# Gate weights split one half-tile a row behind long exponentials, and queries loaded a head ahead, in a one-core conformer layer

## The chip, the cores and the metric

The kernel runs on one core of a Trainium2 chip. The metric is the device time of one execution in microseconds (us), lower is better. Three executions of the kernel before took 1444.28, 1443.33 and 1444.24 us, with a median of 1444.24 us.

## The reference

The kernel computes one inference step of a hybrid streaming encoder layer in float32: a prompt of 1024 frames and 32 new frames of a running stream with 512 cached keys. Model width 1024, 8 heads of 64, a convolution branch of 512 channels, and a feed-forward width of 4096.

```python
p = x @ w_in            # [GLU pair | q | k | v | forget logits | branch gates 2*1024]
u = a * sigmoid(b);  y_conv = swish(LN(causal depthwise conv_31(u))) @ w_conv_out
c = cumsum(log_sigmoid(p_f + b_f))
s = q @ k.T / 8 + c_q - c_k;  s = where(k_pos <= q_pos, s, -1e30)
o = softmax(s) @ v;  y_attn = o @ w_attn_out
mix = (sigmoid(g_conv) * y_conv + sigmoid(g_attn) * y_attn) @ w_o
x1 = LN1(alpha * x + mix);  x2 = LN2(alpha * x1 + relu(x1 @ w_up)**2 @ w_down)
```

## The kernel before

Every float32 matrix is split into a high and a low part, and a product is three matrix products that are summed in PSUM: high by high, high by low, low by high (`mm3`). So a weight tile of 128 x 1024 must be split before TensorE (PE) can use it. The class `Weights` (object `W`) does that. It loads a tile as two raw halves of 128 x 512 (names `raw60`, `raw61`, ...; four raw buffers), and for each half ScalarE (ACT) copies the high part (`whi30`) and another engine subtracts it from the raw half to get the low part (`wlo30`). During the attention that engine is GpSimd (POOL): `W.engine = "pool"`. Four tiles of parts can be held (`RB = 4`). `W.take` gives the next tile to a consumer and splits what is not yet split.

The order of the instructions on PE, ACT, VectorE (DVE) and POOL is written out by the kernel itself: class `Issue` (object `I`) keeps a modelled clock for each engine and emits instructions in the order in which the Python code reaches them. The order of SyncE's (SP's) transfers is set by the framework's scheduler. `I.service` is called after each group of work and first calls `I.always`, which is `W.ahead`: it loads raw halves as buffers allow and splits every half that has arrived and has a place.

The attention is the stage of `with pool("b")`. Its work units are 8 prompt heads with 8 rows each and 4 cached streams (two heads each, 544 keys), which stand behind heads 2, 3, 4 and 5. Row r (class `Rows`) is a block of 128 queries against n = (r + 1) * 128 keys, so a row has 128 to 1024 keys. The loop over units is a software pipeline of four stages. In one turn the newest row `a0` gets its scores on PE (`ps_s_<head>_<row>`, keys `k1`, `k2` and queries `q1`, `q2`) and its minimum on DVE; the row three turns back, `a3`, gets its product with v on PE (`ps_pv<head>_<pair>`, for odd rows), which ACT (`oa`, `ob`) and POOL (`oh`, `ol`) then drain; `a2` is transposed on PE (`ps_tr_<head>_<row>_<first key tile>`) and copied to its high part on ACT (`th`); `a0` gets its exponential on ACT (`p`, in `weigh`); `a1` is scaled by the reciprocal row sum on DVE (`p<-p,rs`, in `norm`); then DVE makes the low part of `a2`'s transposes (`tl`). The service call ends the turn.

PSUM has two buffers for scores (tag `s`), two shared by the transposes and the products with v (tag `tr`), and two for the gates (tag `acc`).

Between these steps PE gets filler: 6 matmuls at a time of the gate tiles 6 to 15 (`ps_g<tile>_<chunk>`) and of two early output tiles (`ps_yc`). `I.fill(needs)` stands ahead of scores, transposes and products. It emits filler while the model says that the needs are not ready, as long as a quota lasts that grows by some 1.7 groups a row. What the fillers take is split by `W` as above.

A cached stream's keys come as a raw array `ckr`. DVE casts its two heads into `k1` (`sk` in the trace), POOL subtracts the cast from it into `k2` (`k<-ckr,sk`), and the values go the same way over ACT and POOL. These steps are a background generator, `parts`, which `Stream.scores` flushes right before the stream's scores.

`load_head` issues a head's transfers, at row 2 of the head (or at the stream) before: `k1` (two transfers of 256 KB), `q1` (two of 256 KB), the low keys in `k2` (256 KB, and a small one), the high queries in `q2` (256 KB, and a small one), and `v` (512 KB). `k1`, `k2` and `v` alternate between two buffers from unit to unit, `q1` and `q2` from head to head. Head 0's transfers go over POOL's queue, all others over SP's.

The lines that decide when a half is split, before:

```python
def ahead(self):
    while len(self.raw) < 2 * self.limit and held["raw"] < RAWB:
        self.load()
    while self.halves < len(self.raw) and I.ready(self.raw[self.halves]) <= I.t["pe"] and \
            (self.halves % 2 or self.halves // 2 in kept or held["parts"] < RB):
        self.split()
        if len(self.raw) < 2 * self.limit:
            self.load()
```

Of the kernel before, what the change touches and what calls it, by code (L numbers as in the profile page):

```python
# [10 lines left out]
F32R = mybir.dt.float32r  # L11
# [6 lines left out]
P = 128  # L18
D = 1024
SEQ = 1024  # L20
# [5 lines left out]
NKS = PAST + DEC  # L26
# [3 lines left out]
H = 8  # L30
DH = 64
# [9 lines left out]
NT = SEQ // P  # L41
# [4 lines left out]
RB = 4  # L46
# [34 lines left out]
class Issue:  # L81
# [116 lines left out]
    def dma(self, out, in_, queue=None):  # L198
        self.run("dma", max(450, Issue.size(out) * out.shape[0] * 4 / 360), [out], [in_])
        out, in_ = (t.bitcast(F32) if t.dtype == F32R else t for t in (out, in_))  # L200
        (queue or self.nc.sync).dma_start(out, in_)
# [10 lines left out]
    def act(self, out, in_, func, bias=None, **kw):  # L212
        aps = [] if bias is None else [bias]
        self.run("act", self.size(in_) * 0.81 + (62 if self.psum(in_) else 103) + 93 * len(aps),
                 [out] + [v for k, v in kw.items() if k == "accum_out"], [in_] + aps)
        if bias is not None:
            kw["bias"] = bias
        self.nc.scalar.activation(out, in_, func, **kw)  # L218
# [5 lines left out]
    def tt(self, out, a, b, op, eng="dve"):  # L224
        n = self.size(out)
        self.run(eng, n * 1.01 + 80 if eng == "dve" else n * 1.97 + 150, [out], [a, b])
        (self.nc.vector if eng == "dve" else self.nc.gpsimd).tensor_tensor(out, a, b, op)  # L227
# [35 lines left out]
def f32(t):  # L263
    return t.bitcast(F32)
# [3 lines left out]
def hybrid_layer(ctx: ExitStack, tc, io):  # L268
    nc = tc.nc
    I = Issue(nc)  # L270
    dma, mm, act, cp, tt, ts, stt = I.dma, I.mm, I.act, I.cp, I.tt, I.ts, I.stt
# [13 lines left out]
    qk_s = {n: tc.dram_tile([H * DH, T], F32, name=f"{n}_s") for n in ("qh", "ql", "kh", "kl")}  # L285
# [27 lines left out]
    NWO = len(plan)  # L313
# [5 lines left out]
    held = dict(raw=0, parts=0)  # L319

    kept = {NWO + m: lambda m=m: [row(7 + m + n, f"{x}_wo{m}") for n, x in enumerate(("whi", "wlo"))] for m in range(1, KD, 2)}

    class Weights:
        def __init__(self):
            self.raw, self.parts, self.taken, self.done, self.halves = [], [], 0, 0, 0
            self.engine, self.limit = "dve", NWO + 1

        def load(self, queue=None):
            i = len(self.raw)
            held["raw"] += 1  # L330
            self.raw.append(ring.tile([P, RW // 2], F32, tag="raw", bufs=RAWB, name=f"raw{i}"))
            w = plan[i // 2]
            n = w.shape[1] // 2
            dma(self.raw[i][:, :n], w[:, i % 2 * n:(i % 2 + 1) * n], queue)
# [17 lines left out]
        def ahead(self):  # L352
            while len(self.raw) < 2 * self.limit and held["raw"] < RAWB:
                self.load()
            while self.halves < len(self.raw) and I.ready(self.raw[self.halves]) <= I.t["pe"] and \
                    (self.halves % 2 or self.halves // 2 in kept or held["parts"] < RB):
                self.split()
                if len(self.raw) < 2 * self.limit:
                    self.load()

        def take(self):
            self.ahead()
            i = self.taken
            while self.halves < 2 * i + 2:
                if len(self.raw) == self.halves:
                    self.load()
                self.split()
            self.taken += 1
            return self.parts[i]
# [6 lines left out]
    class Sums:  # L376
# [18 lines left out]
        def step(self):  # L395
            n = self.n
            self.n += 1
            u, o = divmod(n + 5, 7)
            if u < len(self.units):
                raw = [self.raw.get((u, i)) for i in range(4)]  # L400
                if o == 2:
                    self.total("s1", u, raw[1], raw[3], ADD)
                    self.total("s2", u, self.sums["s1", u], raw[0], SUB)
                if o == 4:
                    self.total("s3", u, raw[0], raw[1], SUB)
                    self.load(u + 1, 0)
                    self.load(u + 1, 1)
                if o == 5:
                    self.total("s4", u, raw[2], self.sums["s2", u], SUB)
                    self.load(u + 1, 2)  # L410
                if (n + 5) % 2 == 0:
                    self.tiles = [ring.tile([P, RW], F32R, tag=x, bufs=RB, name=f"s{x}{n + 5}") for x in ("whi", "wlo")]
                m = (n + 5) % 2 * 512
                self.parts[n + 5] = [t[:, m:m + 512] for t in self.tiles]
                self.src[n + 5] = raw[0] if o == 0 else raw[2] if o == 1 else raw[3] if o == 6 else                     self.sums[(0, 0, "s2", "s1", "s3", "s4")[o], u]
                act(self.parts[n + 5][0], self.src[n + 5], AF.Copy)
            if n + 4 in self.parts:
                hi, lo = self.parts[n + 4]
                tt(lo, self.src[n + 4], f32(hi), SUB)
                if (n + 4) % 7 == 6:  # L420
                    self.load((n + 4) // 7 + 1, 3)
            return self.parts.pop(n, None)

    W = Weights()
# [28 lines left out]
    def row(i, name, dtype=F32R):  # L453
        return xp.tile([P, T], dtype, tag=f"x{i}", bufs=1, name=name)
# [387 lines left out]
    with pool("b") as pb, pool("pb", space=PSUM) as psb:  # L842
        k2s, q2s = [], []
# [11 lines left out]
        crows = [c_s[2 * i:2 * i + 2].rearrange("s (t h) i -> h s t i", h=H) for i in range(2)]  # L855
# [4 lines left out]

        def load_head(h, i):
            hr = slice(h * DH, (h + 1) * DH)
            k1 = pb.tile([P, 2 * NKS], F32R, tag=f"k1{i % 2}", bufs=1, name=f"k1_{h}")
            q1 = pb.tile([P, SEQ], F32R, tag=f"q1{h % 2}", bufs=1, name=f"q1_{h}")
            k2, q2 = k2s[i % 2], q2s[h % 2]
            v = pb.tile([P, 10, P], F32R, tag=f"v{i % 2}", bufs=1, name=f"v_{h}")
            queue = nc.gpsimd if h == 0 else None
            dma(k1[0:DH, 0:SEQ], qk_s["kh"][hr, 0:SEQ], queue)  # L870
            dma(k1[DH:P, 0:SEQ], qk_s["kh"][hr, 0:SEQ], queue)
            dma(q1[0:DH], qk_s["qh"][hr, 0:SEQ], queue)
            dma(q1[DH:P], qk_s["ql"][hr, 0:SEQ], queue)
            dma(k2[0:DH, 0:SEQ], qk_s["kl"][hr, 0:SEQ], queue)
            dma(k2[DH:DH + 2, 0:SEQ].rearrange("s (t i) -> s t i", i=P), crows[0][h, :, 0:NT, :], queue)
            dma(q2[0:DH], qk_s["qh"][hr, 0:SEQ], queue)
            dma(q2[DH + 2:DH + 4, :].rearrange("s (t i) -> s t i", i=P), crows[1][h, :, 0:NT, :], queue)
            dma(v[:, 0:NT, :], v_s[h])
            return k1, k2, q1, q2, v

# [200 lines left out]
        class Stream:  # L1081


            def __init__(self, ops, g):
                self.ops, self.g = ops, g

            def scores(self):
                k1, k2, q1, q2, _ = self.ops
# [46 lines left out]
        def work():  # L1135
            for n, (kind, h) in enumerate(units):
                ops = loaded.pop(n)
                if kind == "cached":
                    load(n + 1)
                    yield Stream(ops, h)  # L1140
                    continue
                for i, r in enumerate(ROWS):
                    if i % 2 == 0:
                        pair = []
                    if i == 2:
                        load(n + 1)
                    yield Rows(ops, h, r, pair)

        act(tiny, eps, AF.Exp)
        a1 = a2 = a3 = None  # L1150
        I.quota = Q0
        for a0 in chain(work(), (None,) * 3):
            I.quota += ((16 - GA + YM / 2) * 12 - Q0) / (H * NT + H // 2)
            if a0:
                a0.scores()
            if a1:
                I.recip(a1.sm[3], a1.sm[3])
            if a3:
                a3.values()
            if a2:  # L1160
                a2.turn()
            if a0:
                a0.weigh()
            if a1:
                a1.norm()
            if a2:
                for r in a2.rest:
                    tt(*r, SUB)
            I.service()
            a1, a2, a3 = a0, a1, a2  # L1170
        act(tiny, eps, AF.Sigmoid)
        while I.step(True):
            pass

# [94 lines left out]
    with pool("ps1", space=PSUM) as bank_pool[0]:  # L1269
        yo = [cbank("yo", "mu", 2)[:, :CB]]  # L1270
        with pool("y") as py:
# [23 lines left out]
            for m in range(YM):  # L1295
                g = g_rows[m][0]
# [504 lines left out]
    for i, cs in enumerate(tail):  # L1801
# [14 lines left out]
        n, s = cs.stop - cs.start, None  # L1816
        for m in range(KD):
# [3 lines left out]
            s = run_sum(cs, m, s, f"n2_{i}")  # L1821
# [8 lines left out]
    n, tag = cs.stop - cs.start, "n2_last"  # L1830
    tiles = [a[:, cs] for a in acc]
    nth, sq, var, s, held_ps = len(turned), [], None, None, {}

    def spare(name):
        return tmp("xr", 3, name)[:, :n]
# [29 lines left out]
    s = spare("lnsum2")  # L1865
# [114 lines left out]
```

## Time and profile before

| | |
|---|---|
| runs of the kernel before | 1444.28, 1443.33, 1444.24 us; median 1444.24 us |
| the profiled execution's own time | 1444.01 us |
| its span from first to last instruction | 1441.4 us |
| mean granted TensorE clock | 0.998 of full speed |
| PE busy in the span | 1425.4 us, 99% |
| PE weight loads (PEld) | 1404.0 us, 97% |
| DVE, ACT, POOL busy | 78%, 47%, 9% |
| the attention with its fillers | about 287 to 569 us of the span |

The profile is one execution, recorded instruction by instruction. A group row gives line, engine, operation, tiles (out<-in), shape and count, then busy time, the mean duration of one in ns, and the idle time ahead of them with what ended most of it. A timeline row gives the start in us, the duration, the engine and the operation, and in brackets the idle time ahead of it and what released it. A row that stands for several instructions shows their count as x4 and the time from the first's start to the last's end. Matmuls overlap one another in these rows, so the distance from one start to the next is what one costs PE. "PEld" is the weight load that runs ahead of a matmul, "SPq" is the issuing of transfers by SP. A row of the waits view gives the waiting group, what it waited for, the total in us, the number of times and the longest. A row of the windows view gives the stretch, its length, and busy time and instruction count of PE, PEld, DVE, ACT and POOL, then the granted clock, the DMA engines' busy share and GB/s. A row of the chain view gives start, duration, engine, group and count.

### The profile page before, as it was taken

How to read it: one execution, taken by the hardware profiler on the slowest of the kernel's cores; microseconds unless marked ns; L12 is line 12 of the kernel's file. 1: busy time of each engine (PE TensorE's matmuls, PEld its weight loads, DVE VectorE, ACT ScalarE, POOL GpSimd, SP SyncE). 2: the span in 40 equal slices, each digit the busy share in tenths (PEclk: the TensorE clock that was granted, in tenths of full speed). 3: DMA queues.
4: the chain of work that ended last, by engine and by line, in shares of the span. 5: the costliest groups of instructions: out<-in, count | busy, mean ns of one | idle time of the engine just before them, and what ended most of it. 6: DMA issues, size and time to landing. Idle time of an engine off the chain costs nothing.

```text
span 1441.4 us, 27988 instructions
## 1 busy us (share of the span) xinstructions
PE 1425.4 (99%) x10623; PEld 1404.0 (97%) x10623; DVE 1119.5 (78%) x1929; ACT 683.0 (47%) x1446; POOL 124.2 (9%) x183
## 2 busy tenths in 40 slices
PE   9999999999999999999999999999999999999996
PEld 8999999999999999999999999999999999999996
DVE  6998899865666655855797888888976789889668
ACT  5123433465665656543345666676657323321134
POOL 0000000023455533000000000000000000000000
PEclk9999999999999999999999999999999999999999
DMA  7125554287455557425343348766689999884212
GB/s 249 46 61 161 171 172 157 88 273 209 111 152 157 154 153 264 144 83 177 94 135 124 130 151 296 251 239 231 225 287 344 335 317 333 276 321 176 67 45 77
DMA packets 157441, 267.91 MB, mean 186 GB/s; under 512 B 22680, under 2 KB 81272, under 8 KB 157308
## 3 DMA queue, kind: packets, MB, share of 16 engines
q1 hardware_dynamic: 156348, 263.98, 55.4%
q0 software_dynamic: 544, 1.59, 0.5%
q8 instruction: 84, 1.38, 0.4%
q10 hardware_dynamic: 416, 0.56, 0.1%
q14 instruction: 49, 0.40, 0.1%
HBM read 168.29 MB, written 97.74 MB: 185 GB/s over the span
## 4 chain that ended last, share of the span: by engine, by line
PE 97%; DVE 1%; DMA 1%; ACT 0%; issue 0%; SPq 0%; DVEq 0%
PE ps_u L206 18%; PE ps_d L206 17%; PE ps_g L206 13%; PE ps_dn L206 6%; PE ps_o L206 6%; PE ps_up L206 5%; PE ps_v L206 3%; PE ps_yc L206 3%; PE ps_k L206 3%; PE ps_glua L206 3%; PE ps_q L206 3%; PE ps_glub L206 3%; PE ps_yo L206 3%; PE ps_s L206 3%; PE ps_pv L206 2%; PE ps_tr L210 2%
## 5 line engine op out<-in xcount | busy, mean ns | idle before, releaser
L235 DVE SCALAR_TENSOR_TENSOR ca<-u,prm,ca 128x1086 f32<-128x1086 f32 x120 | 161.7, 1347 | 2.4
L206 PE MATMUL ps_g<-xh,whi 128*128 128x352 f32 x384 | 131.7, 343 | 0.0
L218 ACT ACTIVATE swhi<-s 128x512 fp32r<-128x512 f32 x100 | 61.9, 624 | 146.9 <-DVE s L227 134.0
L206 PE MATMUL ps_g<-xh,wlo 128*128 128x352 f32 x384 | 123.7, 322 | 0.0
L206 PE MATMUL ps_g<-xl,whi 128*128 128x352 f32 x384 | 121.5, 322 | 0.0
L206 PE MATMUL ps_u<-tl,swhi 128*128 128x264 f32 x416 | 118.4, 285 | 0.0
L206 PE MATMUL ps_u<-th,swhi 128*128 128x264 f32 x416 | 118.2, 284 | 0.0
L206 PE MATMUL ps_u<-th,swlo 128*128 128x264 f32 x416 | 118.2, 284 | 0.0
L218 ACT ACTIVATE whi<-raw 128x512 fp32r<-128x512 f32 (+1 forms) x120 | 69.6, 624 | 69.6 <-PE ps_glua L206 29.7
L227 DVE TENSOR_TENSOR tl<-ps_tr,th 128x512 fp32r<-128x512 f32 (+2 forms) x96 | 51.4, 552 | 60.2 <-ACT th L218 59.5
L206 PE MATMUL ps_d<-hu_h,swhi 128*128 128x264 f32 x480 | 93.0, 285 | 0.1
L206 PE MATMUL ps_d<-hu_l,swhi 128*128 128x264 f32 x480 | 92.9, 285 | 0.0
L218 ACT ACTIVATE r<-r 128x528 f32<-128x528 f32 (+1 forms) x120 | 73.9, 616 | 37.8 <-DVE r L227 35.5
L227 DVE TENSOR_TENSOR wlo<-raw,whi 128x512 fp32r<-128x512 f32 (+1 forms) x100 | 64.8, 686 | 29.1 <-ACT whi L218 28.9
L227 DVE TENSOR_TENSOR r<-r,ps_u 128x528 f32<-128x528 f32 x91 | 62.6, 699 | 29.6 <-PE ps_u L206 29.6
L206 PEld LDWEIGHTS ps_u<-th,swhi 128*128 128x128 f32 x416 | 78.3, 188 | 0.0
L206 PEld LDWEIGHTS ps_u<-th,swlo 128*128 128x128 f32 x416 | 78.3, 188 | 0.0
L206 PEld LDWEIGHTS ps_u<-tl,swhi 128*128 128x128 f32 x416 | 78.2, 188 | 0.0
L227 POOL TENSOR_TENSOR acc<-acc,lnrest 128x288 f32<-128x288 f32 x4 | 3.0, 787 | 857.6 <-ACT lnrest L218 857.6
L206 PEld LDWEIGHTS ps_d<-hu_h,swhi 128*128 128x128 f32 x480 | 74.6, 189 | 0.3 <-issue 0.2
L206 PEld LDWEIGHTS ps_d<-hu_l,swhi 128*128 128x128 f32 x480 | 74.6, 189 | 0.0
L206 PEld LDWEIGHTS ps_g<-xh,whi 128*128 128x128 f32 x384 | 72.7, 189 | 0.7
(434 smaller groups left out, 4997.8 us busy)
## 6 DMA issues: line engine op xcount, KB each, us to landing
h_s<-sp SPq DMA_DIRECT2D x84, 528.0 KB
raw<-in_w_in_dram SPq DMA_DIRECT2D x63, 256.0 KB
hu_h<-h_s SPq DMA_DIRECT2D x30, 528.0 KB
hu_l<-h_s SPq DMA_DIRECT2D x30, 528.0 KB
sraw<-in_w_up_dram SPq DMA_DIRECT2D x52, 256.0 KB
hu<-h_s SPq DMA_DIRECT2D x24, 528.0 KB
sraw<-in_w_ds_dram SPq DMA_DIRECT2D x48, 256.0 KB
g_s<-gt SPq DMA_DIRECT2D x48, 176.0 KB
```

The lines of the kernel that those rows point to most:

```text
L206: self.nc.tensor.matmul(ps, lhsT=w, rhs=x, start=start, stop=stop)
L210: self.nc.tensor.transpose(ps, x, ident)
L218: self.nc.scalar.activation(out, in_, func, **kw)
L227: (self.nc.vector if eng == "dve" else self.nc.gpsimd).tensor_tensor(out, a, b, op)
L235: self.nc.vector.scalar_tensor_tensor(out, a, s, b, op0, op1)
```

## The change

Two things are changed, both in the attention.

First, during the attention's loop `W.paced` is true. Then `ahead` only loads raw halves, and splits are made one half at a time by `W.step`, right behind a row's exponential, if that row has more than 256 keys (rows 2 to 7 and the cached streams). `take` still splits what its tile lacks. Behind the loop `paced` is false again.

Second, the queries' four transfers of head h + 1 are issued at row 2 of head h, ahead of the next unit's loads. `load_head` loads keys and values alone, and takes the queries from there. Where a cached stream stands between two heads, the queries thereby come one unit earlier than before in the program text. Head 0's queries are loaded with its keys on POOL's queue, as before.

```diff
@@ class Weights
+            self.engine, self.limit, self.paced = "dve", NWO + 1, False
         def ahead(self):
             while len(self.raw) < 2 * self.limit and held["raw"] < RAWB:
                 self.load()
-            while self.halves < len(self.raw) and I.ready(self.raw[self.halves]) <= I.t["pe"] and \
-                    (self.halves % 2 or self.halves // 2 in kept or held["parts"] < RB):
+            while not self.paced and self.step():
+                pass
+
+        def step(self):
+            i = self.halves
+            if i < len(self.raw) and I.ready(self.raw[i]) <= I.t["pe"] and (i % 2 or i // 2 in kept or held["parts"] < RB):
                 self.split()
                 if len(self.raw) < 2 * self.limit:
                     self.load()
+                return True
+            return False
@@ the attention
+        def load_queries(h, queue=None):
+            hr = slice(h * DH, (h + 1) * DH)
+            q1 = pb.tile([P, SEQ], F32R, tag=f"q1{h % 2}", bufs=1, name=f"q1_{h}")
+            q2 = q2s[h % 2]
+            dma(q1[0:DH], qk_s["qh"][hr, 0:SEQ], queue)
+            dma(q1[DH:P], qk_s["ql"][hr, 0:SEQ], queue)
+            dma(q2[0:DH], qk_s["qh"][hr, 0:SEQ], queue)
+            dma(q2[DH + 2:DH + 4, :].rearrange("s (t i) -> s t i", i=P), crows[1][h, :, 0:NT, :], queue)
+            queries[h] = q1, q2
@@ load_head
-            dma(q1[0:DH], qk_s["qh"][hr, 0:SEQ], queue)
-            dma(q1[DH:P], qk_s["ql"][hr, 0:SEQ], queue)
+            if h == 0:
+                load_queries(h, queue)
+            q1, q2 = queries[h]
...
-            dma(q2[0:DH], qk_s["qh"][hr, 0:SEQ], queue)
-            dma(q2[DH + 2:DH + 4, :].rearrange("s (t i) -> s t i", i=P), crows[1][h, :, 0:NT, :], queue)
@@ work
                     if i == 2:
+                        if h + 1 < H:
+                            load_queries(h + 1)
                         load(n + 1)
@@ the loop over units
+        W.paced = True
...
             if a0:
                 a0.weigh()
+                if a0.n > 2 * P:
+                    W.step()
...
+        W.paced = False
```

`Stream` gets `self.n = NKS` (544) for the test. Each engine has the same instructions as before, with the same counts; their order differs.

On PE, ahead of the scores of head 7's row 6, the row before the change (`ps_yc0_1` is filler, the second third of the first early output tile):

```order
L206 MATMUL ps_s_7_5_6945<-bfs_264 128x128
L210 MATMUL ps_tr_7_3_0_6956<-ident_130,p_7_3_6854 128x128 x4
L206 MATMUL ps_s_7_6_6965<-k1_7_6399,q1_7_6400 128x512
L206 MATMUL ps_s_7_6_6965<-k2_1_3585,q2_1_3587 128x512
L206 MATMUL ps_s_7_6_6965<-k1_7_6399,q1_7_6400 128x384
```

and now:

```order
L206 MATMUL ps_s_7_5_6945<-bfs_264 128x128
L210 MATMUL ps_tr_7_3_0_6956<-ident_130,p_7_3_6884 128x128 x4
L206 MATMUL ps_yc0_1_6966<-ysh0_6731,whi36_5832 128x352
L206 MATMUL ps_yc0_1_6966<-ysl0_6735,whi36_5832 128x352
L206 MATMUL ps_yc0_1_6966<-ysh0_6731,wlo36_5833 128x352
L206 MATMUL ps_yc0_1_6966<-ysh1_6732,whi36_5832 128x352
L206 MATMUL ps_yc0_1_6966<-ysl1_6736,whi36_5832 128x352
L206 MATMUL ps_yc0_1_6966<-ysh1_6732,wlo36_5833 128x352
L206 MATMUL ps_s_7_6_6965<-k1_7_6432,q1_7_6423 128x512
```

Six filler matmuls stand between the transposes and the scores, where none stood.

On PE, between the two halves of the transposes of head 5's row 6, before (`ps_g14_0` is filler, the first third of gate tile 14):

```order
L206 MATMUL ps_pv5_2_6239<-tl5_4_4_6127,v_5_5695 128x128
L210 MATMUL ps_tr_5_6_0_6265<-ident_130,p_5_6_6089 128x128 x4
L206 MATMUL ps_g14_0_6206<-xh6_144,whi34_5046 128x352
L206 MATMUL ps_g14_0_6206<-xl6_152,whi34_5046 128x352
L206 MATMUL ps_g14_0_6206<-xh6_144,wlo34_5047 128x352
L206 MATMUL ps_g14_0_6206<-xh7_145,whi34_5046 128x352
L206 MATMUL ps_g14_0_6206<-xl7_153,whi34_5046 128x352
L206 MATMUL ps_g14_0_6206<-xh7_145,wlo34_5047 128x352
L210 MATMUL ps_tr_5_6_4_6273<-ident_130,p_5_6_6089 128x128 x3
```

and now:

```order
L206 MATMUL ps_pv5_2_6276<-tl5_4_4_6154,v_5_5715 128x128
L210 MATMUL ps_tr_5_6_0_6302<-ident_130,p_5_6_6115 128x128 x4
L210 MATMUL ps_tr_5_6_4_6310<-ident_130,p_5_6_6115 128x128 x3
L206 MATMUL ps_s_6_0_6319<-k1_6_6207,q1_6_5938 128x128
L206 MATMUL ps_s_6_0_6319<-k2_0_3568,q2_0_3570 128x128
```

The six filler matmuls between the two groups of transposes are gone from this place. The same happens at the transposes of stream 2 (`ps_str2_0`, `ps_str2_4`), behind `ps_pv4_3`. The fillers that left these places stand earlier in the program: ahead of the scores of streams 1, 2 and 3 there are now 54, 42 and 36 filler matmuls where there were 24 each time, and ahead of head 3's first scores 18 where there were 30.

On POOL, around the subtraction of stream 3's cached keys (`k2_1<-ckr3`), before:

```order
L227 TENSOR_TENSOR ol_5_1_6113<-oa_5_1_6107,oh_5_1_6112 64x256
L227 TENSOR_TENSOR k2_1_3585<-ckr3_5934,sk1_3_5921 64x512 x2
L227 TENSOR_TENSOR sv_3_5922<-cvr3_5936,sv_3_5922 128x4x64 x2
L227 TENSOR_TENSOR wlo37_6197<-raw74_5385,whi37_6196 128x512
L227 TENSOR_TENSOR wlo37_6197<-raw75_5389,whi37_6196 128x512
```

and now:

```order
L227 TENSOR_TENSOR ol_5_1_6140<-oa_5_1_6134,oh_5_1_6139 64x256
L227 TENSOR_TENSOR wlo37_6166<-raw74_5517,whi37_6165 128x512
L227 TENSOR_TENSOR wlo37_6166<-raw75_5537,whi37_6165 128x512
L227 TENSOR_TENSOR k2_1_3585<-ckr3_5956,sk1_3_5943 64x512 x2
L227 TENSOR_TENSOR sv_3_5944<-cvr3_5958,sv_3_5944 128x4x64 x2
```

The two halves of tile 37 now stand ahead of the stream's keys. Stream 1 has the same change, with tile 34. At streams 0 and 2 no half stands right ahead of the keys. On SP, the two transfers of head 4's `q1` stood 20 and 16 rows ahead of its `k1` before, and stand 30 and 27 rows ahead now. On ACT, the high halves of tiles 30 to 39 stood in pairs, right behind each other; now each stands right behind an exponential of 384 keys or more.

More of the change, by code (lines that the diff above doesn't have):

```diff
@@ L325, in __init__ @@
             self.raw, self.parts, self.taken, self.done, self.halves = [], [], 0, 0, 0
-            self.engine, self.limit = "dve", NWO + 1
+            self.engine, self.limit, self.paced = "dve", NWO + 1, False
         def load(self, queue=None):
@@ L859, in bbank @@
             return psb.tile([P, 512], F32, tag="acc", bufs=2, name="ps_" + name)
+        queries = {}
+        def load_queries(h, queue=None):
[7 more added lines that the diff above has]
+            queries[h] = q1, q2
         def load_head(h, i):
@@ L865, in load_head @@
             k1 = pb.tile([P, 2 * NKS], F32R, tag=f"k1{i % 2}", bufs=1, name=f"k1_{h}")
-            q1 = pb.tile([P, SEQ], F32R, tag=f"q1{h % 2}", bufs=1, name=f"q1_{h}")
-            k2, q2 = k2s[i % 2], q2s[h % 2]
+            k2 = k2s[i % 2]
             v = pb.tile([P, 10, P], F32R, tag=f"v{i % 2}", bufs=1, name=f"v_{h}")
@@ L1084, in __init__ @@
             def __init__(self, ops, g):
-                self.ops, self.g = ops, g
+                self.ops, self.g, self.n = ops, g, NKS
             def scores(self):
```

## Prediction

> **What bounds the kernel now.** First the page: the totals, the clock, and the chain that ended last by engine.
>
> ```profile
> span 1441.4 us, 27988 instructions
> PE 1425.4 (99%) x10623; PEld 1404.0 (97%) x10623; DVE 1119.5 (78%) x1929; ACT 683.0 (47%) x1446; POOL 124.2 (9%) x183
> ...
> PEclk9999999999999999999999999999999999999999
> ...
> PE 97%; DVE 1%; DMA 1%; ACT 0%; issue 0%; SPq 0%; DVEq 0%
> ```
>
> PE is busy 1425.4 of 1441.4 us at full clock, and 97% of the chain is PE. The change moves work of ACT, POOL and SP and the places of PE's filler, and adds none. So the next view is that of what PE waits for, over the whole span.
>
> ```profile
> PE ps_warm L542 <- DVE warm L537: 1.2, 1, 1.2
> PE ps_glub L206 <- ACT xh L218: 1.1, 2, 0.7
> PE ps_s L206 <- ACT p L218: 0.6, 1, 0.6
> PE ps_o L206 <- DVE wlo_wo L227: 0.6, 1, 0.6
> PE ps_tr L210 <- DVE tl L227: 0.4, 1, 0.4
> PE ps_yo L206 <- DVE yg L227: 0.4, 1, 0.4
> PE ps_glub L206 <- DVE xl L227: 0.2, 1, 0.2
> ```
>
> All waits of PE sum to 4.5 us. Only two lie in the attention, 1.0 us: scores behind an exponential (0.6), transposes behind `tl` (0.4). Neither names a half (`whi`, `wlo`) or a transfer. The windows show the attention (287 to 569) beside a stretch of the projections.
>
> ```profile
> 100.00:200.00 100.00, 100.00 (x735) 99.98 (x734) 88.73 (x133) 39.99 (x104) 0.00 (x0) 1.00 0.52 164
> 286.90:569.40 282.50, 281.50 (x1935) 267.77 (x1934) 173.26 (x360) 171.97 (x416) 118.14 (x162) 1.00 0.62 180
> ```
>
> PE is busy 281.50 of 282.50 us. ACT has 172 us and POOL 118 us of work, so both have room, and what matters of their order is only whether PE is ever made to wait by it.
>
> **The change part by part.** *The halves themselves.* Twenty halves move, each with one copy on ACT and one subtraction on POOL:
>
> ```profile
> L227 POOL TENSOR_TENSOR wlo<-raw,whi 128x512 fp32r<-128x512 f32 x20 | 26.6, 1348 | 27.9 <-ACT whi L218 27.9
> L218 ACT ACTIVATE whi<-raw 128x512 fp32r<-128x512 f32 x26 | 14.9, 628 | 0.0
> ```
>
> Before, a pair kept ACT for 2 x 0.63 = 1.26 us ahead of whatever drain came next (`oa`, `ob`, `th`); now a half keeps it for 0.63. Nothing on PE waited for a drain behind a pair, since the two waits above are elsewhere, so the removal pays 0. Can a half now be late for PE? While stream 3's filler reads `whi34`, POOL is already at `wlo37`: three tiles ahead. The chain of waits prices a filler matmul:
>
> ```profile
> 404.61 4.77 PE ps_g L206 x30
> ```
>
> 4.77 / 30 = 0.159 us each, 0.95 for six. A tile feeds 3 x 24 = 72 of them, 11.4 us, so three tiles are some 34 us of PE work even without the rows between. A half that comes a few rows later stays hidden; without this cover each tile would cost 0.63 + 1.35 = 2.0 us. I take 0.
>
> *Filler into a stall.* The order puts six fillers ahead of the scores of head 7's row 6. There stands the larger of the two waits:
>
> ```profile
> 549.22 0.65 PE L210 MATMUL ps_tr<-ident,p 128*128 128x128 f32 x4
> ...
> 549.57 0.79 ACT L218 ACTIVATE p<-ps_s,mn 128x640 f32<-128x640 f32 x1
> ...
> 550.50 0.50 PE L206 MATMUL ps_s<-k,q 128*128 128x512 f32 x1 [0.63 <-ACT p L218]
> ```
>
> The scores need the buffer that row 4's exponential reads until 550.36, and start 0.14 later. The four transposes start at 549.22; the next quoted four (at 402.70, below) free PE after 0.38, so PE is free at about 549.6 and stands until 550.50, 0.9 us less what the four cost here (bounds 0.63, the row's own figure, and 0.9). Six fillers are 0.95, which fills it. I take -0.8.
>
> *Filler taken from between two transposes.* At two places (head 5's row 6, stream 2) the second group of transposes loses its six fillers. It needs the `tr` buffer of the product with v just ahead, which ACT reads twice (`oa`, `ob`). The same sequence with fillers, at stream 0:
>
> ```profile
> 402.70 0.62 PE L210 MATMUL ps_tr<-ident,p 128*128 128x128 f32 x4
> ...
> 402.96 0.38 ACT L218 ACTIVATE oa<-ps_pv 64x256 f32<-64x256 f32 x1 [0.89 <-PE ps_pv L206]
> ...
> 403.08 0.41 PE L206 MATMUL ps_g<-xh,whi 128*128 128x352 f32 x1
> ...
> 403.36 0.38 ACT L218 ACTIVATE ob<-ps_pv 64x256 f32<-64x256 f32 x1
> ...
> 404.12 0.49 PE L210 MATMUL ps_tr<-ident,p 128*128 128x128 f32 x3
> ```
>
> PE is free for the second group at 403.08; `ob` ends at 403.74, and with the 0.14 of the exponential's release above PE would start at 403.88: 0.8 us bare. The bound below is 0 (if ACT gets to `oa` before PE ends the first group), above 1.4 (a half of 0.63 ahead of `oa`). The rows have ACT idle 0.89 ahead of `oa`, so the middle: 0.8 each, +1.6 for two.
>
> *One cover gone in head 6.* Ahead of its last product with v stood eight fillers:
>
> ```profile
> 539.57 1.52 PE L206 MATMUL ps_g<-xl,whi 128*128 128x352 f32 x8
> ...
> 540.00 0.69 DVE L227 TENSOR_TENSOR tl<-ps_tr,th 128x512 fp32r<-128x512 f32 x1 [0.82 <-ACT th L218]
> ...
> 540.93 0.28 PE L206 MATMUL ps_pv<-th,v 128*128 128x256 f32 x1
> ...
> 541.04 0.28 PE L206 MATMUL ps_pv<-tl,v 128*128 128x256 f32 x1
> ```
>
> Without them the product can start at some 539.6, and the `tl` that it needs is ready at 540.69. If the wait stands at the first matmul that is 1.1; but the low part of the second group of keys is first read by the tenth matmul (four key tiles take two each), and by the starts 540.93 and 541.04 nine of them take 9 x 0.11 = 1.0 us, so nearly all is covered. Bounds 0 and 1.1, and I take 0.2, near the covered end, since the two groups are tiles of their own.
>
> *Keys of the streams behind halves.* At streams 1 and 3 two halves now precede the keys' subtraction on POOL, and the casts on DVE come at the flush:
>
> ```profile
> 496.17 2.94 POOL L227 TENSOR_TENSOR k<-ckr,sk 64x512 fp32r<-64x512 f32 x2
> ...
> 500.28 0.39 PE L206 MATMUL ps_ss<-k,sq 128*128 128x512 f32 x1
> ...
> L222 DVE CAST sk<-ckr 128x512 fp32r<-128x512 f32 x8 | 3.0, 411 | 0.0
> ```
>
> At stream 3 the keys are ready at 499.11 and read at 500.28: 1.2 us to spare. Two halves and two casts make them 2 x 1.35 + 2 x 0.41 = 3.5 later. The twelve more fillers ahead of the scores push the reader back by 12 x 0.159 = 1.9, so 3.5 - 1.9 - 1.2 = 0.4 could show. But the halves delay the keys only if POOL has not done them before the casts, and the first product reads only the first of the two subtractions, so the price lies from 0 to 0.4, and I take 0. At stream 1 thirty more fillers are 4.8 us, more than 3.5: 0.
>
> *Loads.* SP's order was free before, and in it head 4's queries already stood 16 to 20 rows ahead of head 4's keys; no wait of PE names a transfer. The move earns 0. It passes the queries' three 256 KB ahead of keys, and head 3's first scores lose 12 fillers of cover:
>
> ```profile
> 400.69 1.99 SPq L201 DMA_DIRECT2D k<-kh_s  x2
> 402.76 0.55 SPq L201 DMA_DIRECT2D k<-kl_s  x1
> ...
> 402.00:404.00 2.00, 2.00 (x18) 2.00 (x18) 0.00 (x0) 1.06 (x4) 2.00 (x2) 1.00 0.53 155
> 404.00:406.00 2.00, 2.00 (x15) 1.98 (x14) 1.25 (x2) 1.55 (x4) 1.85 (x4) 1.00 1.01 234
> ```
>
> The three key transfers are asked for by 403.3; by 406 the queues have moved (155 + 234) x 2 = 778 KB, about what was asked. The scores, at 404.61 + 4.77 = 409.4, come at 407.5 without twelve fillers. That leaves 1.5 us, so 0, with 1.9 as the bound if other transfers went first.
>
> **Sum.** -0.8 + 1.6 + 0.2 + 0 + 0 = +1.0 us against the profiled execution's 1444.01: 1445.0. The median of the runs, 1444.24, is 0.2 above that execution, so this is +0.8, or 0.05%. About 0.2% (2.9 us: 1441.35 to 1447.13) is what a measurement of this kernel can tell from no change.
>
> **The rivals.** *Faster by half of the weight-load gap.* In the attention PEld is busy 267.77 / 282.50 = 94.8%, in the projections 99.98%: 14.7 us in which no weights are loaded. If those were hidden stalls that pacing halves, the kernel would take 1444 - 7 = 1437. Against it: the waits give 1.0 us to PE here, and the scores' matmuls of 512 columns last 421 ns against a weight load of 188 to 190 ns, so PEld rests while PE works.
>
> ```profile
> L206 PE MATMUL ps_s<-k,q 128*128 128x512 f32 x96 | 31.3, 421 | 0.6 <-ACT p L218 0.6
> ```
>
> [...]
>
> *Slower by POOL meeting the scalings.* A subtraction on POOL that now starts behind an exponential meets the next scaling (`norm`) on DVE. One such meeting in the timeline, and the group of these scalings:
>
> ```profile
> 393.54 2.65 POOL L227 TENSOR_TENSOR k<-ckr,sk 64x512 fp32r<-64x512 f32 x2 [1.51 <-DVE sk L222]
> 394.90 1.70 DVE L231 TENSOR_SCALAR p<-p,rs 128x768 f32<-128x768 f32 x1
> 397.26 0.33 PE L210 MATMUL ps_tr<-ident,p 128*128 128x128 f32 x1 [0.36 <-DVE tl L227]
> ...
> L231 DVE TENSOR_SCALAR p<-p,rs 128x768 f32<-128x768 f32 x8 | 6.0, 751 | 0.2
> ```
>
> That scaling took 1.70 us, and the other seven of its size average (6.0 - 1.70) / 7 = 0.61. It ended 0.4 after POOL did. The transposes and `tl` behind it came later, and PE stood 0.4 to 0.5: the second of the two waits. If half of the twenty halves now do this at 0.55 each, that is +5.5: 1450. It decides from six such meetings on (6 x 0.55 = 3.3). Against it: the 26.6 us of halves also ran beside DVE before, in 173 of 282 us of DVE work, and brought no wait, since the fillers took the delay.
>
> The Trainium skill ("SBUF — State Buffer", Who interferes with whom) says that VectorE in a two-port mode and GpSimd lock one another out of a shared port pair for a whole instruction, scalings included; the trace agrees with 1.70 against 0.61.
>
> *Slower by a queue.* Keys that are late behind halves on POOL at streams 1 and 3, and raw loads that wait for a half ahead of head 4's keys on SP. If fillers run out there, each costs up to the two halves of 2.7 us: two give +5.4, so 1449. It decides when the quota is empty at the stream; the order shows more fillers there, not fewer.
>
> *The loads do nothing.* As argued, the second part may change no wait at all. Then the time is the forecast's.
>
> **How the numbers follow.** The forecast, small terms on both sides of zero, 0.81, in which the loads do nothing in 0.6 of all and something inside the bounds in 0.21; the weight-load rival 0.05; POOL 0.08; the queue 0.06. The forecast's own bounds: below -0.9 and nothing else, with a further 0.5 if the second wait goes, 1442.6; above -0.6 + 2.8 + 1.1 + 0.4, 1447.7, and the 1.9 of the loads would come on top of that only rarely. As the slower rivals hold more than the faster, the range is 1442.5 to 1447.8. Faster by over 0.2%: 0.05. Slower: the 0.08 and 0.06, and 0.01 from the forecast's upper end: 0.15. Same: 0.80.
>
> **What would show it.** In the changed profile: the wait of `ps_s` for `p` at head 7 gone; two waits of `ps_tr` for `ob` of some 0.7 us each, in head 5 and at stream 2; no wait of PE for `whi`, `wlo` or a transfer; PE busy in the attention within 1 us of 281.5. The POOL rival would show as more scalings far above 0.61 with `ps_tr` waits behind them, the queue rival as `ps_ss` or `ps_s` waiting for `k` or a transfer. I am wrong if the waits of PE in the attention sum to over 3 us, or if the time falls by more than the 1.0 us that PE waited there.

## The result

The changed kernel takes 1450.58 us, the median of five runs (1450.03 to 1451.93), against 1444.24 before: 1.0045 times as long, with a 95% interval of 1.0033 to 1.0058. It is slower by 6.3 us. The forecast was 1445.0, with 1442.5 to 1447.8 as the range, so the forecast is wrong; the rival of POOL meeting the scalings, at 0.08, gave 1450.

The page of the changed kernel, the same three lines as of before:

```profile
span 1449.0 us, 27998 instructions
...
PE 1428.1 (99%) x10623; PEld 1405.3 (97%) x10623; DVE 1131.8 (78%) x1929; ACT 682.7 (47%) x1446; POOL 122.7 (8%) x183
...
PE 93%; DVE 4%; DMA 1%; ACT 1%; issue 1%; POOL 1%; DVEq 0%; ACTq 0%; POOLq 0%
```

The chain now has 4% of DVE in place of 1%, and DVE is busy 12 us longer with the same instructions. The attention window, up to 0.3 us behind the last product with v as before:

```profile
286.90:576.40 289.50, 283.90 (x1935) 268.07 (x1934) 185.27 (x361) 171.90 (x416) 116.58 (x162) 1.00 0.60 176
```

The same 1935 matmuls take 289.5 us instead of 282.5; 0.4 of the 7.0 was there ahead of the first scores (330.31 instead of 329.86), so 6.6 are lost inside. The rest of the program is about as long as it was. What PE waits for in the whole span, the rows that lie in the attention:

```profile
PE ps_tr L210 <- DVE p L231: 2.4, 3, 0.8
...
PE ps_tr L210 <- DVE tl L227: 0.9, 1, 0.9
PE ps_pv L206 <- DVE tl L227: 0.9, 4, 0.2
PE ps_tr L210 <- ACT ob L218: 0.5, 1, 0.5
PE ps_str L210 <- ACT ob L218: 0.5, 1, 0.5
...
PE ps_ss L206 <- POOL k L227: 0.3, 1, 0.3
```

They sum to 5.5 us, against 1.0 before. The scores' wait for `p` at head 7 is gone. Three waits of 0.8 are transposes behind a scaling, and four are products that wait for `tl`, which DVE makes behind a scaling. The wait of 0.9 is at head 2, where a scaling of 768 keys meets the two subtractions of the cached keys and takes 2.90 us instead of 1.70; no half is involved there, and the wait was 0.4 before. So 4.5 of the 6.6 us show as waits; in the rest PE counts as busy, 283.90 us instead of 281.50. The groups by form of the attention say why:

```profile
L227 POOL TENSOR_TENSOR wlo<-raw,whi 128x512 fp32r<-128x512 f32 x20 | 25.7, 1289 | 21.4 <-PE ps_tr L210 16.9 <-ACT whi L218 4.5
...
L231 DVE TENSOR_SCALAR p<-p,rs 128x384 f32<-128x384 f32 x8 | 10.0, 1251 | 0.3
...
L231 DVE TENSOR_SCALAR p<-p,rs 128x512 f32<-128x512 f32 x8 | 8.9, 1117 | 0.3
```

and the same two groups of scalings in the kernel before:

```profile
L231 DVE TENSOR_SCALAR p<-p,rs 128x512 f32<-128x512 f32 x8 | 5.2, 653 | 0.3
...
L231 DVE TENSOR_SCALAR p<-p,rs 128x384 f32<-128x384 f32 x8 | 4.0, 495 | 0.3
```

The scalings of rows 2 and 3 take 9.7 us more in sum, 1251 ns instead of 495 and 1117 instead of 653. POOL's subtractions take no longer than they did (1289 ns, 1348 before). One such place, row 3 of head 1 in the timeline of the changed kernel:

```profile
362.34 2.52 POOL L227 TENSOR_TENSOR wlo<-raw,whi 128x512 fp32r<-128x512 f32 x2
...
362.98 2.16 DVE L231 TENSOR_SCALAR p<-p,rs 128x512 f32<-128x512 f32 x1
...
365.29 0.30 PE L210 MATMUL ps_tr<-ident,p 128*128 128x128 f32 x1 [0.81 <-DVE p L231]
```

and the same scaling and its transposes before:

```profile
363.09 0.49 DVE L231 TENSOR_SCALAR p<-p,rs 128x512 f32<-128x512 f32 x1
...
364.46 0.63 PE L210 MATMUL ps_tr<-ident,p 128*128 128x128 f32 x4
```

Before, the scaling ended at 363.58, 0.88 us ahead of its transposes. Now two halves are on POOL, the scaling ends at 365.14, 0.28 behind the second of them (364.86), and is 1.67 longer. 0.88 of that is hidden, and PE stands for the rest, 0.81.

### The profile page after: what moved, and what is told of

Its sections match the earlier page's. It is cut to its first block, busy times and chain, and to the rows that moved or that the text cites. A ratio compares the mean times of both kernels' runs of the same rounds, so it can differ in the third digit from the quotient of the medians.

```text
span 1449.0 us, 27998 instructions
## 1 busy us (share of the span) xinstructions
PE 1428.1 (99%) x10623; PEld 1405.3 (97%) x10623; DVE 1131.8 (78%) x1929; ACT 682.7 (47%) x1446; POOL 122.7 (8%) x183
## 4 chain that ended last, share of the span: by engine, by line
PE 93%; DVE 4%; DMA 1%; ACT 1%; issue 1%; POOL 1%; DVEq 0%; ACTq 0%; POOLq 0%
PE ps_u L206 18%; PE ps_d L206 16%; PE ps_g L206 11%; PE ps_dn L206 6%; PE ps_o L206 6%; PE ps_up L206 5%; PE ps_v L206 3%; PE ps_glub L206 3%; PE ps_k L206 3%; PE ps_glua L206 3%; PE ps_q L206 3%; PE ps_yc L206 3%; PE ps_yo L206 3%; PE ps_pv L206 2%; PE ps_tr L210 2%; PE ps_s L206 2%
## 5 line engine op out<-in xcount | busy, mean ns | idle before, releaser
L235 DVE SCALAR_TENSOR_TENSOR ca<-u,prm,ca 128x1086 f32<-128x1086 f32 x120 | 161.8, 1348 | 2.4
```

Source lines behind the costliest of these rows:

```text
L235: self.nc.vector.scalar_tensor_tensor(out, a, s, b, op0, op1)
```

## The experiments

Two theories stood. The **meeting theory** puts the loss on POOL's subtractions of halves that run into DVE's scalings of rows 2 and 3. The **filler theory** puts it on the fillers that left their places, and on the new order as such.

### One part at a time

`queries_alone` has the second part only:

```diff
-        W.paced = True
...
-                if a0.n > 2 * P:
-                    W.step()
```

> The change's second part without the first: queries a head ahead, halves split in pairs as before. Two theories stand. Meeting theory: the loss is made where a half's subtraction on POOL, now behind an exponential of 384 or 512 keys, runs into DVE's scaling of a row (2.16 and 1.80 us instead of about 0.65 and 0.50 in the changed kernel's trace), and PE waits for it. Filler theory: the loss comes from the fillers that left their places (two bare transposes, stream 3's late keys) and from what else the new order does. By the order, this kernel has one of the two bare transposes (head 5) and the fillers ahead of head 7's row 6, with the halves where they were. Meeting theory: 1444.2 + 0.64 - 0.84, so about 1444, between 1443.3 and 1445.0. Filler theory: most of the loss, 1447 to 1450.

Measured: 1448.26 us, 1.0029 (1.0018 to 1.0041). The meeting theory's number is missed by 4 us. The waits of PE and the timeline at head 3's first scores:

```profile
PE ps_s L206 <- DMA k<-c_s: 1.1, 1, 1.1
...
PE ps_s L206 <- DMA k<-kh_s: 0.6, 1, 0.6
```

```profile
400.42 2.00 SPq L201 DMA_DIRECT2D k<-kh_s  x2
402.51 0.55 SPq L201 DMA_DIRECT2D k<-kl_s  x1
...
406.14 0.30 PE L206 MATMUL ps_s<-k,q 128*128 128x128 f32 x1 [0.61 <-DMA k<-kh_s]
...
407.50 0.30 PE L206 MATMUL ps_s<-k,q 128*128 128x128 f32 x1 [1.07 <-DMA k<-c_s]
```

The keys are asked for when they were before (400.69 and 402.76 there), but PE is at the scores 3 us sooner, since in this kernel's order 6 fillers stand ahead of them where 30 stood. So there is a second cause. These waits are 1.7 of the 4.0 us; the largest others, 0.5 each, are the bare transposes of head 5 and transposes behind a scaling of 256 keys, which in this order meets two halves (1.76 us at 521.52). The filler theory's range is met, at a place that it had not named.

`pacing_alone` has the first part only: `load_head` as in the kernel before, and no `load_queries`.

> The change's first part without the second: one half a row behind exponentials of 384 keys or more, queries loaded with the keys as before. By the order there is no bare transpose, and the halves of heads 0, 1, 2, 4 and 5 stand behind the exponentials of rows 2 and 3. Meeting theory: most of the loss, 1447.5 to 1450, with scalings of 384 and 512 keys that average over 1 us and waits of ps_tr for p and of ps_pv for tl. Filler theory: no loss, 1443.5 to 1445, since no place has lost its cover.

Measured: 1450.00 us, 1.0041 (1.0028 to 1.0053), as the meeting theory has it. Its waits of PE and its groups:

```profile
PE ps_pv L206 <- DVE tl L227: 2.3, 6, 0.7
PE ps_tr L210 <- DVE p L231: 1.6, 2, 0.8
```

```profile
L231 DVE TENSOR_SCALAR p<-p,rs 128x384 f32<-128x384 f32 x8 | 10.0, 1253 | 0.3
L231 DVE TENSOR_SCALAR p<-p,rs 128x512 f32<-128x512 f32 x8 | 8.3, 1039 | 0.3
```

Alone the two parts lose 4.0 and 5.8 us, together 6.3 and not 9.8. The change has 18 fillers ahead of head 3's first scores, not 6, and PE's stalls behind the meetings give the keys time: no wait for a key shows in the change.

### Taking the meetings away

`low_by_dma` is the changed kernel with

```diff
-            tt(lo, raw, f32(hi), SUB, self.engine)
+            if self.engine == "pool":
+                I.run("pool", n * 1.97 + 150, [lo], [raw, hi])
+                nc.sync.dma_start(f32(lo), raw)
+            else:
+                tt(lo, raw, f32(hi), SUB, self.engine)
```

> The changed kernel with its orders on PE, ACT and DVE unchanged, but a half's low part in the attention is no longer subtracted by POOL: a transfer on SP's queue copies the raw half to its place. It leaves out the subtraction of these 20 halves (their low parts hold the raw weights). Meeting theory: three waits of ps_tr of 1.0 us and five of ps_pv of 0.3 to 0.4 go, some 4.8 us, so 1450.6 - 4.8 = 1445.8, between 1445 and 1447; the bare transposes (0.64 each), stream 3's keys and the one scaling that meets the cached keys stay. Filler theory: the orders are the same, so 1449.5 to 1451.

Measured: 1446.77 us, 1.0022 (1.0013 to 1.0032): with the same order on PE, ACT and DVE 3.8 us of the loss are gone. Its groups, and what PE now waits for instead:

```profile
L231 DVE TENSOR_SCALAR p<-p,rs 128x384 f32<-128x384 f32 x8 | 3.9, 492 | 0.3
L231 DVE TENSOR_SCALAR p<-p,rs 128x512 f32<-128x512 f32 x8 | 3.9, 487 | 0.3
```

```profile
PE ps_s L206 <- DMA k<-c_s: 0.7, 1, 0.7
PE ps_str L210 <- ACT ob L218: 0.5, 1, 0.5
PE ps_tr L210 <- ACT ob L218: 0.5, 1, 0.5
...
PE ps_s L206 <- DMA k<-kh_s: 0.4, 1, 0.4
...
PE ps_s L206 <- DMA k<-kl_s: 0.3, 1, 0.3
```

The scalings of 512 keys are back at 0.49 us, which they take where nothing runs on POOL. Those of 384 keys take 0.42 alone; four of the eight still meet a short POOL step of a stream. The time is 1 us above the point expected, because waits for keys come out, 1.4 in all: 0.7 at head 3, and 0.7 at head 6. At head 3 the meetings had covered it: the last key transfer is asked for at 402.87 and read at 407.05, 4.2 us later, and in the change at 404.88 and some 4.8 later. At head 6 two copies of halves stand right ahead of the keys' transfers on SP's queue (501.35, 502.63), and whether they make those waits is not shown.

As PE's order is the same in both kernels, the starts of its matmuls can be compared one by one. The changed kernel falls behind `low_by_dma` by 2.7 us at three transposes of row 3 (heads 1, 2 and 7), by 2.3 at five products whose `tl` stands behind a scaling of row 2 (heads 0, 3, 4, 5 and 6), by 0.7 at the cached keys of head 2 and by 0.5 at stream 3's keys. It makes up 2.0 at the keys for which only `low_by_dma` waits. So the meetings with halves cost the change 5.0 us.

`pacing_dma` is the same edit on `pacing_alone`.

> Pacing alone (1450.0 us) with the same orders on PE, ACT and DVE, but the low part of a half in the attention is a transfer's copy of the raw half instead of POOL's subtraction. It leaves out the subtraction of these 20 halves. Meeting theory: all of the loss goes but the one scaling that meets the cached keys, 1444 to 1445. ACT theory: the loss comes from where the high halves now stand on ACT, ahead of th, oa and ob, which this leaves as it is: 1448 to 1450.

Measured: 1443.09 us, 0.9993 (0.9984 to 1.0002), the same as before within the measurement. All 5.8 us of pacing's loss hang on POOL's subtractions; no cost of the high halves' new places on ACT shows.

### Doubling them, and moving them

`pacing_twice` does each subtraction of `pacing_alone` a second time:

```diff
             tt(lo, raw, f32(hi), SUB, self.engine)
+            if self.engine == "pool":
+                nc.gpsimd.tensor_tensor(lo, raw, f32(hi), SUB)
```

> Pacing alone with each subtraction of a half in the attention done twice on POOL, one right behind the other; all other orders the same. It computes the same. Meeting theory: a scaling that meets a half waits until POOL has done both, 1.28 us more each. Pacing alone has about nine places where PE waited behind such a meeting, so 8 to 13 us more: 1458 to 1463, with scalings of 384 and 512 keys around 3 us. If PE's waits came from elsewhere, 1450 to 1452.

Measured: 1454.19 us, 1.0068 (1.0056 to 1.0081): 4.2 more than pacing alone, and not 8 to 13. The timeline shows what was wrong with the expectation:

```profile
362.98 1.27 POOL L227 TENSOR_TENSOR wlo<-raw,whi 128x512 fp32r<-128x512 f32 x1
...
363.62 0.92 DVE L231 TENSOR_SCALAR p<-p,rs 128x512 f32<-128x512 f32 x1
364.33 1.35 POOL L351 TENSOR_TENSOR wlo<-raw,whi 128x512 fp32r<-128x512 f32 x1
```

and the same place of pacing alone, where two halves follow one another:

```profile
361.99 2.51 POOL L227 TENSOR_TENSOR wlo<-raw,whi 128x512 fp32r<-128x512 f32 x2
...
362.64 2.15 DVE L231 TENSOR_SCALAR p<-p,rs 128x512 f32<-128x512 f32 x1
```

The repeated subtraction writes the tile of the first and starts 0.08 us behind its end (364.25, 364.33). In that gap the scaling gets in: it ends at 364.54, having waited for one subtraction. In `pacing_alone` the two halves do not depend on one another and leave no gap at this place, and the scaling waits for both. So the added work does not hold this scaling twice as long; here it even waits less. The loss comes from other places: from later scalings (three waits of `ps_tr` for `p`, 0.7 each), from one wait of 1.5 for `tl`, and from two of 1.0 for `ob`, where POOL gets to `ol`, for which ACT waits, behind the repeated subtraction.

`rows67` is the changed kernel with halves only behind the longest rows and the streams:

```diff
-                if a0.n > 2 * P:
+                if a0.n > 6 * P or a0.n == NKS:
```

> The changed kernel with another bound: a half is split only behind exponentials of more than 768 keys (rows 6 and 7) and of the cached streams. By the order four transposes are bare instead of two, at stream 2 and in heads 3, 4 and 5. Meeting theory: rows 6 and 7 have longer products and more PE work between a scaling and its transposes, and the halves that stand there in the changed kernel (heads 3 and 5) met nothing, so the scalings' waits go and four bare transposes of 0.64 remain: 1444.2 + 2.6 - 0.84 + about 0.5 for the cached keys, so 1446.5, between 1445 and 1447.5. Filler theory: two more bare transposes than in the change, 1451 to 1452.5.

Measured: 1448.46 us, 1.0028 (1.0017 to 1.0040), 1 us above the upper end of the meeting theory's range and 2.5 below the other's. A meeting at a long row, the scaling's group, and PE's waits:

```profile
345.99 1.29 POOL L227 TENSOR_TENSOR wlo<-raw,whi 128x512 fp32r<-128x512 f32 x1 [0.43 <-ACT whi L218]
...
346.45 1.31 DVE L231 TENSOR_SCALAR p<-p,rs 128x896 f32<-128x896 f32 x1
```

```profile
L231 DVE TENSOR_SCALAR p<-p,rs 128x896 f32<-128x896 f32 x8 | 10.3, 1290 | 0.3
```

```profile
PE ps_tr L210 <- DVE tl L227: 1.4, 1, 1.4
PE ps_tr L210 <- ACT ob L218: 1.4, 3, 0.5
...
PE ps_ss L206 <- POOL k L227: 0.6, 2, 0.3
```

The scalings of 896 keys now meet a half (1290 ns), yet no row names `p`: behind a long row PE has enough to do. That these waits go was expected, but by a wrong reading: it said that halves at such rows had met nothing, and in the change two scalings of 896 keys take 1.3 us beside a half, where 0.69 is usual. What is left are the four bare transposes (with the stream's), two late keys of streams, and one wait of 1.4 at head 2, where the scaling meets the cached keys' two subtractions; it was 0.4 before, and that growth was not expected.

`pacing_dve` is `pacing_alone` with the subtraction on DVE, as its last work in a turn:

```diff
+            if self.paced:
+                I.run("pool", n * 1.97 + 150, [lo], [raw, hi])
+                self.late.append((lo, raw, f32(hi)))
...
+        def lows(self):
+            for lo, raw, hi in self.late:
+                nc.vector.tensor_tensor(lo, raw, hi, SUB)
...
+            W.lows()
             I.service()
```

> Pacing alone (1450.0 us), and the low part of a half is subtracted by DVE, as the last thing that DVE does in a turn (behind tl), in place of POOL; the next raw load is issued there too. It computes the same, with the same orders on PE and ACT. Meeting theory: no subtraction of a half on POOL is left to meet a scaling, so the loss goes, as it did with transfers in its place (1443.1); DVE's 0.69 us behind tl may show at a few short rows: 1444, between 1442.8 and 1446. If DVE has no room behind tl: ten halves behind rows 2 and 3 at up to 0.69 each, 1447 to 1450.

Measured: 1461.37 us, 1.0121 (1.0106 to 1.0136), the worst of all, and far outside the first expectation.

```profile
PE ps_pv L206 <- DVE tl L227: 6.8, 9, 1.2
PE ps_tr L210 <- DVE p L231: 5.1, 5, 1.1
```

```profile
L358 DVE TENSOR_TENSOR wlo<-raw,whi 128x512 fp32r<-128x512 f32 x20 | 16.0, 800 | 12.3 <-ACT whi L218 12.3
```

No half is on POOL, but DVE waits 12.3 us for the high halves and works 16.0 on the low ones, all in front of the next row's minimum and scaling. The kernel is 17.9 us longer, and 14.2 of that are PE's waits in the attention. The short rows have no room on DVE, neither for a scaling that waits nor for more work. It is not a meeting, but the same slack is overdrawn; how much of it is DVE's waiting and how much its added work, the run does not separate.

### The second cause

`queries_model` is `queries_alone` with the kernel's modelled transfer clock put back:

```diff
+                            clock = I.t["dma"]
                             load_queries(h + 1)
+                            I.t["dma"] = clock
...
+            if h:
+                I.t["dma"] += 3 * 64 * 1024 * 4 / 360 + 450
```

> Queries a head ahead, halves in pairs as before, and the kernel's own model of the transfers is told that nothing changed: its transfer clock is put back behind the early queries and advanced by their cost where they stood. The orders on PE, ACT and DVE are then those of the kernel before, instruction by instruction; only SP's order differs. Queries alone took 1448.26 us. Planner theory: that loss came from the model, which thinks the keys arrive sooner and so moves 24 of the 30 fillers away from head 3's first scores (and others to the streams), while the keys land when they did: 1444.2, between 1443.3 and 1445.0, and no wait of PE for a key. Transfer theory: the queries ahead on SP delay the keys and raw halves themselves: 1446 to 1448.5 still, with scores waiting for k.

Measured: 1444.64 us, 1.0004 (0.9995 to 1.0013), no change. Of the two waits for keys nothing is left; PE's waits in the attention are those of before:

```profile
PE ps_s L206 <- ACT p L218: 0.6, 1, 0.6
PE ps_tr L210 <- DVE tl L227: 0.4, 1, 0.4
```

So no cost of the early queries as transfers shows; the interval allows up to 1.9 us. What cost 4 us was the order that the model makes when it believes that the keys then come sooner. SP had already put the queries early, so the keys could not come sooner, and the fillers that covered them, and the transposes of head 5, were sent elsewhere.

`both_mended` joins this with `pacing_dve`.

> The whole change without what the two causes need: halves paced behind exponentials with the subtraction on DVE at the end of the turn, queries a head ahead with the model's transfer clock put back. The orders on PE, ACT and DVE are those of the run with DVE and the queries as before; only SP's order differs. If the two causes are all that made the change slower: the same time as that run within 0.7 us, 1443 to 1446. If the early queries themselves cost something on SP, 1 to 2 us above it.

Measured: 1461.49 us, 1.0123 (1.0106 to 1.0140), 0.1 from `pacing_dve`: again no cost of the early queries themselves shows. The time expected, 1443 to 1446, was missed with that of `pacing_dve`. No run is faster than the kernel before by more than its interval, and the waits of before leave only 1.0 us in the attention to gain.

## Why the prediction was wrong

*The halves, taken at 0.* This is the step that failed. It asked whether a half can be late for the filler that reads it, and found three tiles of cover, which held: no wait names `whi` or `wlo`. It asked what is queued behind a half on ACT, which held too (`pacing_dma`). It did not ask here what a subtraction on POOL does to DVE, but left that to a rival whose price, 0.55 a meeting, came from the one meeting at a stream. The rival, with a chance of 0.08, was right in mechanism: in place of 0 the halves cost 5.0 us in the change (`low_by_dma`), and pacing alone lost 5.8. That its total fits so well (1450 for 1450.58) is luck in part. It took ten meetings at 0.55; the runs show three of 0.7 to 1.0 and five of 0.4 to 0.5, and the total also holds the bare transposes, the late keys of stream 3 and the cached keys of head 2.

The rival's counterargument failed: that halves had run beside DVE before without a wait said that the scalings they met then had slack, not that all have. The trace of before even held a scaling of a short row that just escaped, in head 3:

```profile
422.67 2.71 POOL L227 TENSOR_TENSOR wlo<-raw,whi 128x512 fp32r<-128x512 f32 x2 [1.31 <-ACT whi L218]
422.81 1.43 DVE L231 TENSOR_SCALAR p<-p,rs 128x512 f32<-128x512 f32 x1
...
424.38 0.41 PE L210 MATMUL ps_tr<-ident,p 128*128 128x128 f32 x2
```

It took 0.94 longer than the usual 0.49, and ended 0.14 ahead of its transposes, as close as the scaling that PE waited for in the change (365.14, 365.29). At head 1 the slack from the end of row 3's scaling (363.58) to its transposes (364.46) was 0.88 us. A scaling that waits for two halves is 1.67 longer, so such a place must cost about 0.8. In six of the eight heads the change puts both halves of a tile behind the exponentials of just these rows, 2 and 3, and in the other two it puts one behind row 2. At three places, row 3 of heads 1, 2 and 7, the scaling waits for both halves; at five, row 2 of the other heads, it is held by one.

*Filler into the stall, -0.8.* Right: the wait of `ps_s` for `p` is gone.

*Two bare transposes, 0.8 each.* Right in place and mechanism: the view has 0.5 each for `ob`. The row of head 5 gives the price:

```profile
513.53 0.62 PE L210 MATMUL ps_tr<-ident,p 128*128 128x128 f32 x4
...
514.63 0.55 PE L210 MATMUL ps_tr<-ident,p 128*128 128x128 f32 x3 [0.47 <-ACT ob L218]
```

From 513.53 four transposes would free PE after 0.38, at 513.91, so 0.7 each.

*Head 6's lost cover, 0.2.* It shows no wait of its own.

*Keys of stream 3, 0, with 0.4 as the upper bound.* The value, 0.3 in PE's waits, was near the bound:

```profile
508.88 2.64 POOL L227 TENSOR_TENSOR k<-ckr,sk 64x512 fp32r<-64x512 f32 x2 [0.36 <-DVE sk L222]
...
511.57 0.50 PE L206 MATMUL ps_ss<-k,sq 128*128 128x512 f32 x1 [0.27 <-POOL k L227]
```

The first product was not late, as the text had argued. The second subtraction ends at 511.52, and its reader, a later product that the text left out, starts at 511.57.

*Loads, 0, with 1.9 as the bound.* Right for the change by luck. The price was real (at head 3 0.7 in `low_by_dma`, 1.7 in `queries_alone`), and the meetings hid it. The text saw the 12 lost fillers there, but took 1.5 us of room from bytes moved, which do not say whose they are.

*The weight-load rival* is refuted: pacing without meetings (`pacing_dma`) is 1.1 us below the kernel before, within the measurement, and not 7. *The queue rival* named the place of stream 3's keys, at a tenth of its price. *That the second part does nothing* fits the transfers, for which no cost shows, and is wrong for the order, since the model moved the fillers.

## What to carry to other kernels

Work that is moved behind one engine's long instruction must be checked against what runs on every engine while it runs, not only against its own readers. For a step on POOL that means each SBUF-to-SBUF operation of DVE that it will overlap, and the slack from that operation to its reader, row by row: here a delay of 1.67 us met a slack of 0.88 at a short row. And where a program orders its work by a model, an edit that only tells the model something else is an edit of the order.

## What the runs showed of the hardware

A scaling on DVE that comes while POOL subtracts waits for the end of the subtraction. With one half under way it takes 0.92 us where it takes 0.49 alone (`pacing_twice`). With two back to back it took 2.15 and waited for both, and a gap of 0.08 us was enough to be let in between. But two back to back do not always hold it for both: the scaling at 422.81 in the kernel before, shown above, ended at 424.24, while POOL's second half ran until 425.38. What decides was not tried.

POOL is not slowed where it comes first (1.27 us). Where a scaling comes first, POOL waits: in the kernel before, a half that started 0.17 us behind a scaling of 1024 keys (349.32 against 349.15) took 1.74, and the scaling its usual 0.75. That is why the 20 halves had a higher mean before. The Trainium skill ("SBUF — State Buffer", Who interferes with whom) speaks of a lock for a whole instruction, which goes to whoever issues first; these rows agree. DVE's `tl`, which reads PSUM and one SBUF operand, is untouched: in `pacing_alone` five of the 48 of the largest shape run beside a half and take 0.68 to 0.69 us, and all 48 average 0.686. DVE's own subtraction, which reads two SBUF operands, is touched: in `pacing_dve` a low half takes 0.69 us while POOL is idle and 0.80 to 1.27 beside POOL's other steps.

The wait behind the cached keys' two subtractions at head 2, which grew from 0.4 to 1.4 us in `rows67`, comes from a scaling that started 0.11 us behind the first of them (393.96 against 393.85) and waited for both, where before it started near the first's end (394.90). The start alone does not decide it: in `low_by_dma` the scaling started 0.10 behind (393.77 against 393.67) and waited for one.
